# Four latent projections accumulated feature tile by feature tile as the inputs arrive

## The chip, the cores and the metric

One core of one Trainium2 chip runs the whole program. The metric is the device time of one execution in microseconds (us); less is better. The engines that matter here are TensorE (PE in the profile, with its weight loads PEld), VectorE (DVE), ScalarE (ACT), GpSimd (POOL), and SyncE (SP), whose queue issues nearly all loads from HBM.

## The reference, cut to what matters

The model is a two-layer decoder trunk on 512 tokens of 1024 features. Only the input projection of the even layer and what it feeds is touched:

```
h = rms_norm(x, ev_norm)                     # x: 512 x 1024
z = h @ w_in                                 # 1024 -> 512 + 256 + 128 + 32
u, cq, ckv, kr = split(z)                    # pooling, query latent, key/value latent, rotary key
y_pool = pool_mixer(u)                       # causal means over 2/4/8/16 tokens, then 128x128 products
q  = rms_norm(cq) @ w_q_up                   # 8 heads x (64 + 32 rotary)
kv = rms_norm(ckv) @ w_kv_up                 # 8 heads x (64 keys + 64 values)
x  = x + concat(y_pool, attention(q, k, v)) @ w_out
```

After it come a cross-attention into 256 memory tokens and a SwiGLU block, then a second layer with a gated recurrence and the same two blocks, and a final norm.

## The kernel before, in words

Activations lie with features on the 128 partitions and the 512 tokens on the free axis, so x is eight tiles of 128x512. Every float32 operand is split into a high part of reduced precision and the rest (`split` for activations, `Weights.get` for weights), and one product is three matmuls: high by high, high by low, low by high (`mm3`, lines 166 to 168, in this order). One output tile of a 1024-wide projection is thus 8 feature tiles x 3 = 24 matmuls of 128x512 into one PSUM bank. There are eight banks: two each of `mm`, `att`, `s` and `tr`.

The norm of the layer is not applied to x first. `setup` multiplies x by the gain only (line 156 on ACT, 157 on DVE) and sums the squares of x over the feature tiles into `ssq` (a square on ACT, lines 243 and 246; an add on POOL, line 247). The factor per token, `rx`, is worked out from `ssq` later (`rstd_cols`: column sums by matmul at line 183, then small DVE operations and one POOL power) and spread over the partitions by `bcast` (line 230) into `R`.

`setup` loads x tile by tile and, after every second tile, one block of `ev_w_in`. A block of this layout is one output tile: 128x1024 numbers, its eight feature tiles side by side (512 KB). Output tile by output tile, `even` makes z[0], z[1] (query latent), z[2] (key/value latent), z[3] (the 32 rotary keys and their swapped halves, twice), and later the four pooling projections in `u_tile`. Each `linear` call therefore needs all eight tiles of x and one block of weights. Raw weight blocks have two buffers, their high and low parts three each.

A table of rotary factors (`rope_table`, lines 371 to 415) is worked out on DVE and ACT from the positions in between. Behind z come the second norms (line 453: sums of squares of z), the latent for keys and values (`ck`, line 459), the rotary key (464 to 477), the pooling tiles, and the attention of four pairs of heads. The cross-attention's keys of the memory are also worked in there (`mem_gained`, `mem_keys`).

The order of the instructions on each engine is made when the program is built, by a planner that follows the program's order with its own estimates of durations and lets a later instruction go ahead of one that is not ready. `tc.issue_after(i)` holds the instructions of its block behind instruction i. On the chip each engine then keeps that order, and so does SP's queue of loads. Before anything arrives, `setup` runs 12 products of ones with ones (line 296).

Of the kernel before, what the change touches and what calls it, by code (L numbers as in the profile page):

```python
# [18 lines left out]
P = 128  # L19
T = 512  # L20
# [48 lines left out]
class Weights:  # L69
    """Streams [n, 128, F] blocks and splits each into float32r high and low parts."""  # L70
# [33 lines left out]
class Trunk:  # L104
# [23 lines left out]
    def pair(self, side, n=T):  # L128
        """High and low parts of an activation tile, from one of the two sides of the activation store."""
        return tuple(self.actp.tile([P, n], F32R, name=self.nm(f"act{side}"), tag=f"act{side}") for _ in range(2))  # L130
# [7 lines left out]
    def bank(self, tag="mm"):  # L138
        """A PSUM bank: mm and att for products, s for scores, tr for transposes and row sums."""
        if tag == "any":  # L140
            self.flip ^= 1
            tag = ("mm", "att")[self.flip]
        return self.psum.tile([P, T], F32, name=self.nm(tag), tag=tag, bufs=BANKS[tag])
# [15 lines left out]
    def mm3(self, out, terms, begin=True, end=True):  # L159
        """out = sum over terms of (wh + wl).T @ (xh + xl), less wl.T @ xl.  # L160

        A sum in pieces has its first one with begin and its last one with end."""
        nc = self.nc
        last = len(terms) - 1
        for i, (wh, wl, xh, xl) in enumerate(terms):
            nc.tensor.matmul(out, wh, xh, start=begin and i == 0, stop=False)  # L166
            nc.tensor.matmul(out, wh, xl, start=False, stop=False)  # L167
            self.mm_ins = nc.tensor.matmul(out, wl, xh, start=False, stop=end and i == last).ins  # L168

    def rstd_cols(self, *sums, inner=None, bank="tr"):  # L170
        """For each (ssq, dim, tiles, scale): [128, tiles] columns of scale * rsqrt(column sums of ssq / dim + eps).

        With inner the squared values are still to be scaled by these columns, and so is what the result scales."""
        nc = self.nc
        ps = self.bank(bank)
        n = sum(s[2] for s in sums)
        v = self.small(8)
        o = 0
        for ssq, dim, nt, _ in sums:
            terms = ssq if isinstance(ssq, tuple) else (ssq,)  # L180
            for t in range(nt):
                for i, a in enumerate(terms):
                    self.sum_ins = nc.tensor.matmul(ps[:, o + t:o + t + 1], a[:, t * P:(t + 1) * P], self.ones[:, 0:1],  # L183
                                                    start=i == 0, stop=i == len(terms) - 1).ins
            o += nt
        o = 0
        if inner is not None:
            sq = self.small(8)
            nc.vector.tensor_mul(sq[:, :inner.shape[-1]], inner, inner)
        for _, dim, nt, _ in sums:  # L190
            if inner is None:
                nc.vector.tensor_scalar(v[:, o:o + nt], ps[:, o:o + nt], 1.0 / dim, EPS, op0=ALU.mult, op1=ALU.add)
            else:
                nc.vector.scalar_tensor_tensor(v[:, o:o + nt], ps[:, o:o + nt], 1.0 / dim, sq[:, :nt],
                                               op0=ALU.mult, op1=ALU.mult)
            o += nt
        if inner is not None:
            nc.vector.tensor_scalar(v[:, :n], v[:, :n], EPS, None, op0=ALU.add)
        r = self.rsqrt(v, n)
        res, o = [], 0  # L200
        for _, _, nt, scale in sums:
            if inner is not None:
                nc.vector.scalar_tensor_tensor(r[:, o:o + nt], r[:, o:o + nt], scale or 1.0, inner,
                                               op0=ALU.mult, op1=ALU.mult)
            elif scale is not None:
                nc.vector.tensor_scalar(r[:, o:o + nt], r[:, o:o + nt], scale, None, op0=ALU.mult)
            res.append(r[:, o:o + nt])
            o += nt
        return res

    def rsqrt(self, v, n):
        """v ** -0.5 of n columns, refined by one step."""
        nc = self.nc
        y, w, r = (self.small(8)[:, :n] for _ in range(3))
        v = v[:, :n]
        nc.gpsimd.tensor_tensor(y, v, self.mhalf[:, :n], op=ALU.pow)
        nc.vector.tensor_mul(w, y, y)
        nc.vector.tensor_mul(w, w, v)
        nc.vector.tensor_scalar(w, w, -0.5, 1.5, op0=ALU.mult, op1=ALU.add)
        nc.vector.tensor_mul(r, y, w)  # L220
        return r

    def bcast(self, cols, nt=NT, bank="tr"):
        """PSUM tile [128, nt*128] with the columns' values along the free axis, on every partition."""
# [14 lines left out]
    def add_square(self, ssq, src, first):  # L239
# [4 lines left out]
        else:  # L244
            sq = self.tmp("t2", n)
            nc.scalar.activation(sq[:, :n], src, AF.Square)  # L246
            nc.gpsimd.tensor_add(ssq[:, :n], ssq[:, :n], sq[:, :n])  # L247
# [4 lines left out]
    def next_norm(self, side, gain, off):  # L252
        """State for the norm that follows a residual update: filled tile by tile."""
# [10 lines left out]
    def linear(self, W, blk, xs, off=0, bank="mm", ps=None, k0=0, k1=None):  # L264
        """One output tile: block blk of W holds its k tiles side by side. With k0 and k1 a piece of the sum."""
# [18 lines left out]
    def setup(self):  # L284
# [6 lines left out]
        # the table of the first functions is loaded before there is data  # L291
        nc.scalar.activation(self.small(1), self.ones[:, 0:1], AF.Square)
        # the array's clock is raised while the first operands are on their way
# [4 lines left out]
        nxt = self.next_norm(0, "ev_norm", 0)  # L298
        self.Win = Weights(self, ins["ev_w_in"], "evin")
        for m in range(KD):  # L300
            xt = self.actp.tile([P, T], F32, name=self.nm("xin"), tag="act1")
            nc.sync.dma_start(xt, ins["xT"][m * P:(m + 1) * P, :])
            self.feed(nxt, m, xt)
            if m in (0, 2, 4, 6):
                self.Win.get(m // 2)
# [17 lines left out]
    def mem_load(self, keys):  # L323
        """The memory, feature tiles of [128, 256], in the place of the keys to come or among the inputs."""
# [9 lines left out]
    def mem_gained(self, layer, pool, tag, keys=True):  # L334
        """The memory's norm with the layer's gain, split: feature tiles [128, 256], high and low."""
# [17 lines left out]
    def mem_keys(self, layer, mg, m0, m1, low=None):  # L353
        """Keys of the memory, [features, memory tokens]."""
# [9 lines left out]
    def rope_table(self, pool, C):  # L364
        """C: rows 0:64 one, 64:96 cos, 96:128 sin with the sign of its half.

        Worked out with 16 frequencies x 8 chunks of the positions on the partitions."""
# [49 lines left out]
    def even(self, nrm, nxt_spec):  # L417
# [4 lines left out]
        with ExitStack() as ctx:  # L422
# [10 lines left out]
            # latents: z[0:2] of the queries, z[2] of keys and values, z[3] rotary keys and their swapped halves  # L433
            z = [self.linear(Win, m, xg, bank="any") for m in range(2)]
            rx, = self.rstd_cols((nrm["ssq"], D, NT, None))
            with tc.issue_after(self.sum_ins):
                z.append(self.linear(Win, 2, xg, bank="any"))
            sq = [self.tmp(t) for t in ("t0", "t0", "t1")]
            cq = []
            for m in range(2):  # L440
# [3 lines left out]
                cq.append((h, l))  # L444
            with tc.issue_after(self.mm_ins):
                z.append(self.linear(Win, 3, xg, bank="any", k1=2))
            R = self.rp.tile([P, T], F32, name=self.nm("R"), tag="R")
            with tc.issue_after(self.mm_ins):
                row = self.bcast(rx)
            nc.scalar.activation(sq[2], z[2], AF.Square)  # L450
            nc.scalar.copy(R, row)
            with tc.issue_after(self.row_ins):
                rq, rk = self.rstd_cols(((sq[0], sq[1]), 256, NT, QKD ** -0.5), (sq[2], P, NT, None), inner=rx)
            with tc.issue_after(self.sum_ins):
                self.linear(Win, 3, xg, ps=z[3], k0=2)
# [14 lines left out]
            # queries and keys of two pairs of heads; rows 64:128 of the keys stay  # L470
# [8 lines left out]
            nc.vector.tensor_mul(CQ, self.bcast(rq), C)  # L479

            # pooling mixer
            def u_tile(g):
                ps = self.linear(Win, 4 + g, xg)
# [29 lines left out]
            # latent attention  # L513
# [22 lines left out]
            def v_pair(wh, wl):  # L536
                """Values of two heads, tokens on partitions."""
# [99 lines left out]
    def cross(self, layer, nrm, nxt_spec, mg=None):  # L637
# [3 lines left out]
        with ExitStack() as ctx:  # L641
# [40 lines left out]
            def scores(hd):  # L682
                """Softmax of one head's scores, queries on partitions, two query tiles side by side."""
# [103 lines left out]
    def odd(self, nrm, nxt_spec):  # L787
# [6 lines left out]
        with ExitStack() as ctx:  # L794
# [6 lines left out]
            # 8 * softplus(-lambda) = 8 * (max(-lambda, 0) + log1p(exp(-|lambda|)))  # L801
# [37 lines left out]
            def act(out, src, fn, **kw):  # L839
                """A function of ScalarE's tables; run() keeps those of a kind together."""  # L840
# [13 lines left out]
            def lru_gates():  # L854
                for hd in range(4):
                    if hd == 0:
                        # the row of the norm's factors comes between the first tiles
# [68 lines left out]
    def tail(self, W, ys, base, side):  # L926
        """The last projection, its residual and the final norm: features on partitions for the first tokens,
        tokens on partitions for the last ones."""
# [38 lines left out]
        def after(n):  # L967
            """The sums and the row of the norm come in between these products."""
# [46 lines left out]
def layout(inputs):  # L1015
# [21 lines left out]
    d["ev_w_in"] = con(mt(np.concatenate([z[:, 512:896], kr, ks, kr, ks, z[:, :512]], axis=1)))  # L1037
# [53 lines left out]
```

## Time and profile before

| what | us |
|---|---|
| median of 3 runs | 1421.28 |
| lowest and highest of the runs | 1419.26 and 1422.52 |
| span of the profiled execution | 1418.8 |
| PE busy in that span | 1384.2 (98%) |
| DVE, ACT, POOL busy | 784.9 (55%), 549.6 (39%), 321.7 (23%) |

The profile is of one execution; its span runs from the first to the last instruction. Nothing else is shown of that execution's own time, so what lies around the span is taken as the median less the span, 2.5 us. "Idle before" in a row is the engine's idle time ahead of the instruction, with what released it. A matmul's own time in a row includes work that overlaps with the next one; the pace is the distance from one start to the next. PEclk is the clock granted to TensorE as a share of its full speed.

### The profile page before, as it was taken

How to read it: one execution, taken by the hardware profiler on the slowest of the kernel's cores; microseconds unless marked ns; L12 is line 12 of the kernel's file. 1: busy time of each engine (PE TensorE's matmuls, PEld its weight loads, DVE VectorE, ACT ScalarE, POOL GpSimd, SP SyncE). 2: the span in 40 equal slices, each digit the busy share in tenths (PEclk: the TensorE clock that was granted, in tenths of full speed). 3: DMA queues.
4: the chain of work that ended last, by engine and by line, in shares of the span. 5: the costliest groups of instructions: out<-in, count | busy, mean ns of one | idle time of the engine just before them, and what ended most of it. 6: DMA issues, size and time to landing. Idle time of an engine off the chain costs nothing.

```text
span 1418.8 us, 16758 instructions
## 1 busy us (share of the span) xinstructions
PE 1384.2 (98%) x6524; PEld 1153.3 (81%) x6524; DVE 784.9 (55%) x1043; ACT 549.6 (39%) x859; POOL 321.7 (23%) x291
## 2 busy tenths in 40 slices
PE   8989999999999999999999989999999999999997
PEld 6878888878888888888887778888888888888887
DVE  7687574456454345344579796445545534453553
ACT  6466553454332232223434555335433312221331
POOL 4586261103110011001234470211121100110112
PEclk8999999999999999999999989999999999999999
DMA  6222162323223233332322334322323333323331
GB/s 208 75 71 79 60 193 79 115 60 118 90 90 104 89 104 92 102 90 93 108 89 90 98 105 154 96 71 91 116 89 93 100 96 98 99 84 111 93 104 60
DMA packets 45326, 140.28 MB, mean 99 GB/s; under 512 B 5568, under 2 KB 10816, under 8 KB 45248
## 3 DMA queue, kind: packets, MB, share of 16 engines
q1 hardware_dynamic: 43808, 137.91, 31.1%
q10 hardware_dynamic: 1440, 1.32, 0.3%
q8 instruction: 51, 0.84, 0.2%
q14 instruction: 27, 0.22, 0.0%
HBM read 136.98 MB, written 2.10 MB: 98 GB/s over the span
## 4 chain that ended last, share of the span: by engine, by line
PE 86%; DVE 7%; issue 2%; ACT 2%; DMA 1%; POOL 1%; POOLq 0%; SPq 0%; ACTq 0%; DVEq 0%
PE mm L166 16%; PE mm L168 16%; PE mm L167 16%; PE att L166 10%; PE att L168 10%; PE att L167 10%; DMA dn_raw<-in_ffn_down_dram 1%; DVE h L896 1%; DVE act L154 1%; PE s L166 1%; PE s L167 1%; PE s L168 1%; DVE i L895 1%; PE tr L183 1%; PE mm L667 1%
## 5 line engine op out<-in xcount | busy, mean ns | idle before, releaser
L98 ACT CAST gu_h<-gu_raw 128x1024 fp32r<-128x1024 f32 x88 | 92.8, 1054 | 293.0 <-PE mm L167 162.7
L774 POOL TENSOR_TENSOR t<-t,t 128x512 f32<-128x512 f32 x44 | 60.0, 1364 | 577.9 <-ACT gu_h L98 383.1
L99 DVE TENSOR_TENSOR gu_l<-gu_raw,gu_h 128x1024 fp32r<-128x1024 f32 x88 | 138.2, 1570 | 33.1 <-ACT gu_h L98 33.1
L166 PE MATMUL att<-act,gu_h 128*128 128x512 f32 x352 | 137.8, 391 | 0.0
L166 PE MATMUL mm<-act,gu_h 128*128 128x512 f32 x352 | 137.1, 390 | 0.0
L168 PE MATMUL att<-act,gu_l 128*128 128x512 f32 x352 | 137.0, 389 | 0.0
L167 PE MATMUL mm<-act,gu_h 128*128 128x512 f32 x352 | 136.9, 389 | 0.0
L168 PE MATMUL mm<-act,gu_l 128*128 128x512 f32 x352 | 136.9, 389 | 0.0
L167 PE MATMUL att<-act,gu_h 128*128 128x512 f32 x352 | 136.9, 389 | 0.0
L247 POOL TENSOR_TENSOR ssq<-ssq,t 128x512 f32<-128x512 f32 (+1 forms) x49 | 77.5, 1582 | 196.5 <-ACT t L246 188.5
L773 DVE TENSOR_TENSOR t<-att,R 128x512 f32<-128x512 f32 x44 | 30.4, 691 | 128.3 <-PE att L168 128.3
L98 ACT CAST dn_h<-dn_raw 128x1024 fp32r<-128x1024 f32 (+1 forms) x40 | 40.3, 1011 | 138.2 <-PE att L167 102.5
L167 PEld LDWEIGHTS att<-act,gu_h 128*128 128x128 f32 x352 | 66.2, 188 | 14.2 <-issue 0.5
L166 PEld LDWEIGHTS att<-act,gu_h 128*128 128x128 f32 x352 | 66.0, 188 | 14.1 <-issue 0.5
L168 PEld LDWEIGHTS mm<-act,gu_l 128*128 128x128 f32 x352 | 66.1, 188 | 13.9
L168 PEld LDWEIGHTS att<-act,gu_l 128*128 128x128 f32 x352 | 66.0, 188 | 13.7
L167 PEld LDWEIGHTS mm<-act,gu_h 128*128 128x128 f32 x352 | 66.0, 187 | 13.7
L166 PEld LDWEIGHTS mm<-act,gu_h 128*128 128x128 f32 x352 | 66.1, 188 | 13.5
L274 DVE TENSOR_TENSOR x<-mm,x 128x512 f32<-128x512 f32 x44 | 30.3, 690 | 83.4 <-PE mm L168 82.6
L770 DVE TENSOR_TENSOR t<-mm,R 128x512 f32<-128x512 f32 x44 | 30.4, 691 | 69.6 <-PE mm L168 66.8
L153 ACT CAST act<-t 128x512 fp32r<-128x512 f32 (+1 forms) x53 | 32.9, 621 | 71.9 <-POOL t L774 56.0
L99 DVE TENSOR_TENSOR dn_l<-dn_raw,dn_h 128x1024 fp32r<-128x1024 f32 (+1 forms) x40 | 56.2, 1408 | 6.6 <-ACT dn_h L98 6.6
(397 smaller groups left out, 3541.8 us busy)
## 6 DMA issues: line engine op xcount, KB each, us to landing
gu_raw<-in_ffn_gu_dram SPq DMA_DIRECT2D x88, 512.0 KB, 3.5
dn_raw<-in_ffn_down_dram SPq DMA_DIRECT2D x32, 512.0 KB, 3.6
xk_raw<-in_xa_w_k_dram SPq DMA_DIRECT2D x16, 512.0 KB, 3.5
xq_raw<-in_xa_w_q_dram SPq DMA_DIRECT2D x16, 512.0 KB, 3.6
xv_raw<-in_xa_w_v_dram SPq DMA_DIRECT2D x16, 512.0 KB, 3.5
xo_raw<-in_xa_w_o_dram SPq DMA_DIRECT2D x16, 512.0 KB, 3.6
odin_raw<-in_od_w_in_dram SPq DMA_DIRECT2D x16, 512.0 KB, 3.5
dn_raw<-in_ffn_down_dram SPq DMA_DIRECT2D x16, 384.0 KB, 3.0
```

The costliest lines, as they stand in the source:

```text
L98: nc.scalar.copy(hi, src)
L99: self.low.tensor_sub(lo, src, hi[:, :].bitcast(F32))
L153: nc.scalar.copy(hi, src)
L154: nc.vector.tensor_sub(lo, src, hi.bitcast(F32))
L166: nc.tensor.matmul(out, wh, xh, start=begin and i == 0, stop=False)
L167: nc.tensor.matmul(out, wh, xl, start=False, stop=False)
L168: self.mm_ins = nc.tensor.matmul(out, wl, xh, start=False, stop=end and i == last).ins
L247: nc.gpsimd.tensor_add(ssq[:, :n], ssq[:, :n], sq[:, :n])
L274: self.nc.vector.tensor_add(self.x[m], ps, self.x[m] if src is None else src)
L770: nc.vector.tensor_mul(t, pg, R)
L773: nc.vector.tensor_mul(u, pu, R)
L774: nc.gpsimd.tensor_mul(u, u, t)
```

## The change

The columns of `ev_w_in` for the four latent tiles get a layout of their own, `ev_z`: eight blocks, one for each feature tile, of 128x512 numbers (256 KB), with the four output tiles side by side. `setup` now runs through the feature tiles: it loads x tile k and block k of `ev_z`, splits both, and issues the 12 matmuls that add this feature tile to all four outputs, which stand open in the two `mm` and the two `att` banks. Three of the eight banks' roles thus change: z[0] and z[2] lie in `mm`, z[1] and z[3] in `att`. In this loop the add of the squares is done by DVE and no longer by POOL.

`even` begins with all four z done. The pooling projections, now blocks 0 to 3 of a smaller `ev_w_in` whose loads and splits are asked for in `even` alone, take the place of z[2] and z[3] as products between which the norms' sums are put: the first three feature tiles of projection 0, then the sums of the second norms, then the other five, then the row of `rx`. Projections 0 and 1 lie in the `s` banks, 2 and 3 in `mm`; 1 to 3 are written down after the rotary keys and before the pooling tiles. The number of matmuls is the same. Comments and docstrings are dropped as well.

```diff
-    def add_square(self, ssq, src, first):
+    def add_square(self, ssq, src, first, low=None):
...
-            nc.gpsimd.tensor_add(ssq[:, :n], ssq[:, :n], sq[:, :n])
+            (low or nc.gpsimd).tensor_add(ssq[:, :n], ssq[:, :n], sq[:, :n])
...
         nxt = self.next_norm(0, "ev_norm", 0)
+        Wz = Weights(self, ins["ev_z"], "evz")
+        Wz.group = 1
+        self.z = [self.bank(t) for t in ("mm", "att") * 2]
+        for k in range(KD):
+            xt = self.actp.tile([P, T], F32, name=self.nm("xin"), tag="act1")
+            nc.sync.dma_start(xt, ins["xT"][k * P:(k + 1) * P, :])
+            h, l = self.pair(0)
+            self.split(xt, h, l, scale=self.vec("ev_norm", k))
+            nxt["xg"].append((h, l))
+            wh, wl = Wz.get(k)
+            for m, z in enumerate(self.z):
+                ms = slice(m * P, (m + 1) * P)
+                self.mm3(z, [(wh[:, ms], wl[:, ms], h, l)], k == 0, k == KD - 1)
+            self.add_square(nxt["ssq"], xt, k == 0, low=nc.vector)
         self.Win = Weights(self, ins["ev_w_in"], "evin")
-        for m in range(KD):
-            xt = self.actp.tile([P, T], F32, name=self.nm("xin"), tag="act1")
-            nc.sync.dma_start(xt, ins["xT"][m * P:(m + 1) * P, :])
-            self.feed(nxt, m, xt)
-            if m in (0, 2, 4, 6):
-                self.Win.get(m // 2)
...
-            z = [self.linear(Win, m, xg, bank="any") for m in range(2)]
+            z, zins = self.z, self.mm_ins
             rx, = self.rstd_cols((nrm["ssq"], D, NT, None))
-            with tc.issue_after(self.sum_ins):
-                z.append(self.linear(Win, 2, xg, bank="any"))
...
+            nc.scalar.activation(sq[2], z[2], AF.Square)
+            R = self.rp.tile([P, T], F32, name=self.nm("R"), tag="R")
+            ups = [self.linear(Win, 0, xg, bank="s", k1=3)]
             with tc.issue_after(self.mm_ins):
-                z.append(self.linear(Win, 3, xg, bank="any", k1=2))
-            R = self.rp.tile([P, T], F32, name=self.nm("R"), tag="R")
+                rq, rk = self.rstd_cols(((sq[0], sq[1]), 256, NT, QKD ** -0.5), (sq[2], P, NT, None), inner=rx)
+            with tc.issue_after(self.sum_ins):
+                self.linear(Win, 0, xg, ps=ups[0], k0=3)
             with tc.issue_after(self.mm_ins):
                 row = self.bcast(rx)
-            nc.scalar.activation(sq[2], z[2], AF.Square)
             nc.scalar.copy(R, row)
-            with tc.issue_after(self.row_ins):
-                rq, rk = self.rstd_cols(((sq[0], sq[1]), 256, NT, QKD ** -0.5), (sq[2], P, NT, None), inner=rx)
-            with tc.issue_after(self.sum_ins):
-                self.linear(Win, 3, xg, ps=z[3], k0=2)
...
             nc.vector.tensor_mul(CQ, self.bcast(rq), C)
+            ups += [self.linear(Win, g, xg, bank="s" if g == 1 else "mm") for g in (1, 2, 3)]
             def u_tile(g):
-                ps = self.linear(Win, 4 + g, xg)
+                ps = ups[g]
...
-    d["ev_w_in"] = con(mt(np.concatenate([z[:, 512:896], kr, ks, kr, ks, z[:, :512]], axis=1)))
+    d["ev_z"] = con(np.concatenate([z[:, 512:896], kr, ks, kr, ks], axis=1).reshape(KD, P, 4 * P))
+    d["ev_w_in"] = con(mt(z[:, :512]))
```

## Rows read from the trace of the kernel before

**Rows 1.** The page: PE's busy time over the whole span, and the granted clock in 40 equal slices of 35.5 us.

```profile
PE 1384.2 (98%) x6524; PEld 1153.3 (81%) x6524; DVE 784.9 (55%) x1043; ACT 549.6 (39%) x859; POOL 321.7 (23%) x291
...
PEclk8999999999999999999999989999999999999999
```

**Rows 2.** The view by windows, the first 98 us cut into seven stretches; its columns are in its first line ("x" counts instructions).

```profile
core 0: us, PE busy (x) PEld busy (x) DVE busy (x) ACT busy (x) POOL busy (x), PEclk, DMA share, GB/s
0.00:6.40 6.40, 5.20 (x25) 5.01 (x25) 0.75 (x2) 3.89 (x6) 2.29 (x17) 1.00 0.67 235
6.40:16.80 10.40, 5.54 (x12) 2.84 (x12) 10.33 (x13) 10.02 (x17) 8.87 (x6) 0.62 0.95 360
16.80:22.60 5.80, 5.76 (x14) 4.56 (x15) 5.80 (x12) 0.57 (x2) 2.40 (x2) 0.50 0.30 90
22.60:28.00 5.40, 5.40 (x27) 4.49 (x25) 3.36 (x9) 1.94 (x5) 0.00 (x0) 1.00 0.47 132
28.00:72.00 44.00, 44.00 (x213) 36.12 (x213) 29.10 (x55) 20.07 (x35) 21.28 (x19) 1.00 0.27 81
72.00:82.00 10.00, 8.04 (x33) 5.75 (x34) 8.47 (x21) 5.88 (x12) 6.93 (x8) 0.83 0.50 167
82.00:98.00 16.00, 13.07 (x85) 10.46 (x83) 15.47 (x32) 11.54 (x32) 13.65 (x17) 1.00 0.00 1
```

**Rows 3.** The timeline of PE in its first 23 us: start, time of one, what it is, and the idle time before it with what ended it.

```profile
0.97 5.13 PE L296 MATMUL tr<-ones 128*128 128x128 f32 x24 [0.97 <-POOL ones L290]
6.33 0.50 PE L166 MATMUL att<-act,evin_h 128*128 128x512 f32 x1 [0.23 <-ACT evin_h L98]
...
8.07 0.50 PE L168 MATMUL att<-act,evin_l 128*128 128x512 f32 x1 [1.00 <-DVE evin_l L99]
...
9.93 0.79 PE L167 MATMUL att<-act,evin_h 128*128 128x512 f32 x1 [1.13 <-DVE act L157]
...
13.14 0.79 PE L167 MATMUL att<-act,evin_h 128*128 128x512 f32 x1 [1.56 <-DVE act L157]
...
16.84 0.80 PE L168 MATMUL mm<-act,evin_l 128*128 128x512 f32 x1 [1.20 <-DVE evin_l L99]
...
22.55 0.45 PE L166 MATMUL mm<-act,evin_h 128*128 128x512 f32 x1
```

**Rows 4.** The chain of work that ended last, in order of time, first 50 us: start, time on the chain, what it is.

```profile
13.01 1.30 DVE rp_l L390
...
15.65 1.14 DVE evin_l L99
...
22.32 0.43 PE mm L168
...
23.23 0.23 PE att L168
...
37.60 0.86 PE tr L230 x2
38.45 2.57 PE tr L183 x24
```

**Rows 5.** The view by windows for PE alone, from the first matmul of z[0] to the end of z[1].

```profile
6.33:27.83 21.50, 16.61 (x49) 0.68 0.65 230
```

**Rows 6.** Groups of DVE instructions between 6 and 28 us, shapes apart: count, busy time in us, mean ns of one, idle before.

```profile
L157 DVE SCALAR_TENSOR_TENSOR act<-xin,vecs,act 128x512 fp32r<-128x512 f32 x7 | 6.2, 887 | 0.0
...
L386 DVE TENSOR_SCALAR rp_q<-rp_r 128x64 f32<-128x64 f32 x1 | 1.3, 1286 | 0.0
...
L382 DVE SCALAR_TENSOR_TENSOR rp_t<-rp_q,rp_t 128x64 f32<-128x64 f32 x3 | 0.6, 210 | 0.0
```

**Rows 7.** Groups of ACT instructions between 3 and 28 us, same columns.

```profile
L156 ACT ACTIVATE act<-xin,vecs 128x512 fp32r<-128x512 f32 x8 | 5.6, 712 | 1.2 <-DMA vecs<-in_vecs_dram 1.2
L246 ACT ACTIVATE t<-xin 128x512 f32<-128x512 f32 x7 | 4.2, 620 | 0.4 <-POOL ssq L247 0.4
```

**Rows 8.** The timeline of ACT and DVE, four single instructions on tiles of 128x512: the low part of the first x tile, a weight block's high part, its low part, and the low part of the values.

```profile
4.64 0.75 DVE L157 SCALAR_TENSOR_TENSOR act<-xin,vecs,act 128x512 fp32r<-128x512 f32 x1 [4.64 <-ACT act L156]
...
60.22 0.62 ACT L98 CAST evp_h<-evp_raw 128x512 fp32r<-128x512 f32 x1
...
62.38 1.12 DVE L99 TENSOR_TENSOR evp_l<-evp_raw,evp_h 128x512 fp32r<-128x512 f32 x1
...
72.38 0.69 DVE L154 TENSOR_TENSOR vl<-att,vh 128x512 fp32r<-128x512 f32 x1
```

**Rows 9.** The issues of DMA up to 70 us: count, KB each, median us from issue to landing.

```profile
xin<-in_xT_dram SPq DMA_DIRECT2D x9, 256.0 KB, 5.2
...
evp_raw<-in_ev_pool_dram SPq DMA_DIRECT2D x1, 256.0 KB, 2.6
```

**Rows 10.** The timeline from 49 to 78 us: the copy of the row for the key/value norm, the low parts of the first two queries, the last matmul of the pooling projections, the first scores, and a matmul of the next pair's queries.

```profile
49.28 0.59 ACT L457 COPY t<-tr 128x512 f32<-128x512 f32 x1 [3.20 <-PE tr L230]
...
65.41 3.03 POOL L526 TENSOR_TENSOR act<-t,act 128x512 fp32r<-128x512 f32 x2
...
69.57 0.39 PE L168 MATMUL mm<-act,evin_l 128*128 128x512 f32 x1
...
71.97 0.53 PE L559 MATMUL s<-act,act 128*128 128x128 f32 x2
...
77.38 0.80 PE L166 MATMUL att<-cqh,evqkv_h 128*128 128x512 f32 x1 [1.00 <-DVE act L154]
```

## The prediction

> **What bounds the kernel now.** I read the page first: PE is busy 98% of the span, and two of the 40 slices show a granted clock below 9 tenths, the first and the twenty-fourth [rows 1]. So the time is PE's own work at its pace, plus what PE loses in a few places. The change keeps the number of matmuls; it can pay only where PE waits or runs slowly. The windows show that place [rows 2]: from 28 to 72 us PE is busy all the time at full clock, whereas from 6.4 to 22.6 us it ran 26 matmuls in 16.2 us at 0.62 and then 0.50 of the clock, that is mostly at 1.2 GHz. The timeline of PE says why [rows 3]. The waits ahead of 8.07, 9.93, 13.14 and 16.84 us are 1.00, 1.13, 1.56 and 1.20 us, each ended by a DVE low part, of a weight block or of an x tile. Behind these waits the clock fell, and it came back only at 22.55, when PE had run without a gap since 16.84. On the chain one matmul goes by in 0.43 us before that and in 0.23 us after [rows 4]. The pace at full clock, from starts that lie next to each other in the trace, is 0.227 us.
>
> DVE is the late one there: 10.33 of 10.40 us busy [rows 2]. Part of that is not work. A rotary-table operation on 128x64 takes 0.21 us by itself and 1.29 us while POOL adds squares [rows 6], and two of these slow ones lead into the weight split that PE then waits for [rows 4].
>
> **What it costs now.** z[0] and z[1] are 48 matmuls; with the first sum they fill 6.33 to 27.83 us [rows 5]. At full pace 48 take 48 x 0.227 = 10.9 us. So 21.5 - 10.9 = 10.6 us are lost there. z[2] and z[3], 48 more, are then done at full pace, so by PE's count all four tiles cost until 27.8 + 10.9 = 38.7 us, leaving aside the sums and rows put in between, which stay.
>
> **The loop of the change, part by part.**
>
> *PE.* Each feature tile now gives 12 matmuls that need only this tile and its block: 12 x 0.227 = 2.72 us at full pace, 12 x 0.43 = 5.2 us at half. Eight tiles are 96 x 0.227 = 21.8 us. The start: the products of ones end at 6.1 us [rows 3], and by then tile 0 is there (below). If nothing waits, z ends at 6.1 + 21.8 = 27.9 us.
>
> *ACT* per tile: the high part of x 0.71, the square 0.62 [rows 7], the high part of a 128x512 block 0.62 [rows 8]: 1.95 us, below 2.72.
>
> *DVE* per tile: the low part of x, the low part of the block, the add of squares. The add and this size of block on DVE are not in the trace without company. Bounds: 0.69 us for the same shape alone, with one operand in PSUM, and 1.12 beside POOL [rows 8]; for the x part 0.75, the time of the first tile, with POOL still idle [rows 8], and the mean of the others, 0.89 [rows 6]. With POOL out of the loop I take the lower ends: 0.75 + 0.69 + 0.69 = 2.13 us, below 2.72. The upper ends give 3.1 us, which would make DVE the bound by 0.4 us a tile. Beside the loop DVE has some 21 rotary operations at 0.21, 4.4 us, and a query weight split of 0.9. In all 8 x 2.13 + 5.3 = 22.3 us against PE's 21.8: the loop's own instructions come first in the program and the rest fills in, so I allow 0.5 us of waiting.
>
> *POOL* loses seven adds and gains nothing; nobody waits for it here.
>
> *Loads.* 16 loads of 256 KB are 4.2 MB against 2.1 MB of x and up to 2.1 MB of weights before. At the 360 GB/s that the loaded queue showed [rows 2] they take 11.7 us, 1.46 us a tile. The narrow place is the two raw buffers: block k + 2 is issued when the low part of block k is done. Landing takes 2.6 us on an empty queue and 5.2 behind others [rows 9]; with 0.62 + 0.69 for the split and about 1 us in DVE's queue a pair of buffers turns in some 4.9 us, 2.5 us a block; behind a full queue, 7.5, or 3.8 a block. SP's queue keeps its order, so the x tiles, the first query weights and the memory's four loads that go ahead of block 2 or 3 delay it. By my count block 2 lands near 9.8 us and is split by 11.3, when PE asks for it at 6.1 + 2 x 2.72 = 11.5; later blocks gain on PE unless the memory's 1 MB (2.9 us) goes in between, a wait of about 1 us at most, since of the 12 matmuls of a tile eight need no low part of the weights. With the 0.5 above I set the end of z at 28.4 us; bounds 27.9 and 33.
>
> **Behind the loop.** Let z end at E. The sums of x (0.8 us), nine matmuls of projection 0 (2.0), the 24 sums of the second norms (2.57, [rows 4]) follow without need to wait: ACT squares z[0] and z[1] while PE still adds the last tile to z[2] and z[3], and 2.8 us are left to it for the rest. The blocks of the pooling weights: the third of them waits only for a buffer freed at E, and there are 2.0 us and more of matmuls between two needs. In the row of before, 8.3 us pass from the end of those sums (41.0) to the copy for the keys' norm at 49.28 [rows 4, 10]; the same chain gives E + 5.4 + 8.3 = E + 13.7. From there the first two queries' low parts on POOL were ready 19.2 us later (68.4 against 49.28, [rows 10]): E + 32.9. PE until then has 0.8 + 2.6 sums, three rows of 0.86, 96 matmuls of pooling and 12 of queries (24.5), so E + 30.5; in the trace of before 2.4 us more go by from the last pooling matmul at 69.57 to the first scores at 71.97, hence E + 32.9. It comes out even; before there was 3.5 us to spare. I charge 0.5 us for this, with up to 2 as the far end. One weight split of 1.2 us on DVE leaves this stretch, since the pooling blocks are split earlier. The waits from 72 to 98 us, where DVE is 15.47 of 16 us busy [rows 2], move along unchanged.
>
> **The sum.** 38.7 - 28.4 - 0.5 = 9.8 us earlier at the attention, and from there on PE is the bound to the end. Against the profiled execution: 1418.8 - 9.8 = 1409.0 of span, plus 2.5 us around it, 1411.5 us; the median of before is that same 1418.8 + 2.5.
>
> **A rule that speaks against it.** After four waits of 1.0 to 1.6 us the granted clock was at 1.2 GHz for some 12 us [rows 3]. The Trainium skill, "TensorE: Matmul & The Clock Gate", section "HAM oscillation — how this bites in real kernels", describes a loop over feature tiles in which each tile's matmuls are short and PE then waits for the next load, so that every tile starts at the low clock; it advises against waiting for data inside such a loop. The trace agrees that waits bring the clock down; whether this loop waits, no row here shows. If that rule decides, it is the third rival.
>
> **Rivals.**
> 1. *DVE sets the pace or the clock falls once.* For it: DVE's total equals PE's; blocks 2 and 3 land just in time. Against: POOL is out of the way. With 3.1 us a tile DVE, which begins at 4.6 [rows 8], ends at about 4.6 + 8 x 3.1 + 2 = 31.4 us; or gaps of 1.5 us and then 14 matmuls at 0.43 instead of 0.227, as between 16.84 and 22.55 [rows 3], 2.8 us, give 32.5. Gain 6 to 7, about 1415 us.
> 2. *The gain is given back before the attention.* The first scores wait for the chain of DVE and POOL behind the rows, and the memory's norm or the rotary table is late as well: PE arrives 10 us early and stands still, falls to the low clock (as at 77.38, [rows 10]) and the time is what it was, 1420 to 1424. For it: the even balance above and DVE's full stretch. Against: nearly all of this chain hangs on z itself, which moves.
> 3. *The loop runs at the low clock from end to end.* PE begins with a tile, waits for the next, and never gets a full stretch: 96 x 0.43 = 41.3 us from 6.1, z at 47.4, against 38.7: 8.7 us slower, 1430. It decides if each tile arrives more than 5.2 us after the one before. Against: at the low clock a tile lasts 5.2 us, longer than any supply worked out above (3.8 at most), so waits end by themselves and the clock returns, as it did at 22.55.
>
> **Chances and range.** The forecast 0.73 (own range 1408 to 1414), rival 1 0.13, rival 2 0.07, rival 3 0.07. The range from 1406.5, where z ends at 27.9 and 4 of the 5 us that PE loses from 72 to 98 go too, to 1418 holds the forecast and rival 1. A difference of less than 0.2% (2.8 us) can't be told from no change: faster 0.86, same 0.07, slower 0.07.
>
> **What would show it.** Right: in the profile after, matmuls into all four z banks from about 6 us at a pace of 0.227 with the clock at 1.00, z done at 28 to 29 us, rotary operations at 0.2 us, the last pooling matmul near 59 instead of 69.57. Wrong: PE waits for the low part of a `ev_z` block or its load, a clock of 0.5 over more than 6 us of the loop, or a new wait of PE between 28 and 60 us, above all before the first scores.

## The result: nothing gained, and the profile after

The changed kernel takes 1423.74 us in the median (1421.61 to 1427.42, 18 runs), the kernel before 1421.3 beside it (18 runs): ratio 1.0019, interval 1.0012 to 1.0026. It is a little slower, 1411.5 was forecast, and the range ended at 1418. The profiled execution spans 1420.9 us, against 1418.8.

The windows of the changed kernel, cut as in [rows 2] up to 28 us and finer behind it:

```profile
6.40:22.60 16.20, 14.73 (x67) 11.61 (x65) 15.20 (x40) 11.02 (x20) 0.00 (x0) 1.00 0.84 276
22.60:28.00 5.40, 5.40 (x28) 4.54 (x28) 2.61 (x12) 3.50 (x8) 1.04 (x1) 1.00 0.61 165
28.00:60.00 32.00, 32.00 (x148) 25.73 (x147) 23.10 (x42) 15.20 (x26) 11.22 (x10) 1.00 0.30 92
60.00:72.00 12.00, 9.37 (x36) 8.09 (x35) 6.90 (x11) 5.18 (x8) 11.26 (x10) 0.69 0.24 72
72.00:84.00 12.00, 8.11 (x32) 5.85 (x32) 8.44 (x22) 5.95 (x13) 5.31 (x7) 0.78 0.22 77
84.00:98.00 14.00, 13.08 (x78) 10.18 (x77) 12.34 (x28) 10.84 (x29) 12.42 (x17) 0.96 0.04 14
```

From 6.4 to 22.6 us PE runs 67 matmuls at full clock instead of 26 [rows 2]: the gain was made. From 60 to 84 us it then idles and runs slowly where [rows 2] show it busy until 72. PE's timeline names the waits. The first line is the last pooling matmul, which started at 69.57 before [rows 10]:

```profile
59.24 0.39 PE L168 MATMUL mm<-act,evin_l 128*128 128x512 f32 x1
...
64.12 0.47 PE L166 MATMUL att<-ckh,evqkv_h 128*128 128x512 f32 x1 [2.63 <-DVE t L530]
...
70.46 0.63 PE L166 MATMUL att<-cqh,evqkv_h 128*128 128x512 f32 x1
...
78.26 0.50 PE L566 MATMUL s<-act,act 128*128 128x512 f32 x1 [1.65 <-ACT pr L640]
...
81.45 0.33 PE L566 MATMUL s<-act,act 128*128 128x128 f32 x1 [2.15 <-ACT pr L640]
```

The view by windows gives the clock behind the first wait (columns: PE busy, clock, DMA):

```profile
64.10:74.70 10.60, 10.58 (x35) 0.52 0.32 111
```

So 2.6 us are lost by waiting, some 5.1 by the half clock and 3.8 by waiting for exps, 11.5 in all. Before, 72 to 82 us lost 10 - 8.04 x 0.83 = 3.3 [rows 2]. The difference, 8.2, is nearly all of what the loop won.

To follow it I add up what PE has started by a time t: each matmul at its pace at full clock (0.227 us for 512 columns, 0.18 and 0.12 for 384 and 256, 0.11 for 128 or fewer). The lead is this sum less that of the kernel before; 8.4 us, say, is 37 matmuls of 512 columns. Beside it stand the starts of the copy for the keys' norm and of the first, seventh and thirty-first exp (eight heads, four rows each; the seventh is the second head's third row). The rows below the second belong to the experiments.

```
lead of PE over the kernel before (us) at t =              | copy  exp 1  exp 7  exp 31
                  30   60   70   85  100  120  145  160  185
before             0    0    0    0    0    0    0    0    0 | 49.3  75.4  88.9  160.6
after            8.4  8.4  2.8 -0.6  0.7  0.7  0.8 -0.8 -2.3 | 47.8  76.0  88.8  162.3
e1 queries 1st   8.6  8.6  3.9 -0.1  1.6  1.6  1.1  0.0 -1.6 | 47.5  74.6  88.5  161.5
e3 squares 1st   8.2  8.4  6.2  3.6  2.5  1.3  0.0 -1.5 -3.0 | 45.5  72.7  92.3  162.9
e4 adds only     2.7  3.0  2.3  1.2  2.8  2.2  1.1  0.1 -1.4 | 46.5  74.2  88.1  161.3
e9 POOL free     8.6  7.0  3.4  2.0  1.9  1.0  0.0 -1.4 -3.0 | 46.9  70.5  92.7  162.9
e10 e3 + casts   8.6  7.0  4.8  3.1  2.0  0.4  0.0  0.0  0.0 | 46.9  74.0  94.4  160.4
e11 all casts    8.6  7.3  3.9  3.3  2.0  1.4  1.1  1.3  1.1 | 46.7  73.9  94.3  159.3
e12 last cast    8.4  6.6  1.8 -1.4 -1.7 -1.4 -1.6 -3.2 -3.2 | 49.6  77.9  91.7  163.8
e14 + mem POOL   8.2  8.4  6.2  3.3  4.3  3.7  1.9  1.7  1.6 | 45.5  72.7  84.6  159.0
e15 + mem PE     8.4  8.4  6.2  3.1  4.8  4.8  3.0  2.8  2.7 | 45.5  72.7  84.5  157.9
e16 all orders   8.4  7.0  4.2  5.1  7.5  7.4  5.7  4.9  5.4 | 47.0  70.1  82.5  155.3
e17 before+ord.  0.2  0.5  0.2  1.2  2.5  1.3  0.4 -1.0 -1.1 | 49.0  76.7  88.2  161.9
e18 no squares   8.2  6.6  1.8  0.1 -0.5 -0.3 -0.4 -2.0 -2.0 | 49.6  73.0  89.9  162.6
```

In the changed kernel 8.4 us are there at 60 us and none at 85, where the exps come when they always came; another 3 go between 145 and 185. The lead at 185 us is what the spans differ by, to 0.7 us, but for e15, which gains 1.8 more later, and e17, whose one execution lost 4 more (mostly behind 700 us, in stages that no edit touches). The expectations below quote leads up to 1 us above this table's.

Each row is one execution, and they scatter: up to 150 us e12 has the order of the changed kernel on every engine, yet its copy comes 1.7 and its first exp 1.9 us later, after a low clock behind 39 us (last section). A landmark that differs by less than 2 us in one execution is weak evidence.

### The profile page after: what moved, and what is told of

The parts are those of the page before. It is cut to its first block, busy times and chain, and to the rows that moved or that the text cites. A ratio compares the mean times of both kernels' runs of the same rounds, so it can differ in the third digit from the quotient of the medians.

```text
span 1420.9 us, 16770 instructions
## 1 busy us (share of the span) xinstructions
PE 1384.6 (97%) x6524; PEld 1153.8 (81%) x6524; DVE 783.3 (55%) x1054; ACT 550.1 (39%) x863; POOL 310.8 (22%) x284
## 4 chain that ended last, share of the span: by engine, by line
PE 84%; DVE 8%; issue 3%; ACT 2%; DMA 2%; POOL 1%; POOLq 0%; ACTq 0%; DVEq 0%
PE mm L166 16%; PE mm L168 16%; PE mm L167 15%; PE att L166 9%; PE att L168 9%; PE att L167 9%; PE s L168 1%; PE s L166 1%; DMA dn_raw<-in_ffn_down_dram 1%; PE s L167 1%; DVE h L903 1%; DVE t L838 1%; DVE i L902 1%; DVE act L154 1%; DVE xk_l L99 1%
## 5 line engine op out<-in xcount | busy, mean ns | idle before, releaser
L247 POOL TENSOR_TENSOR ssq<-ssq,t 128x512 f32<-128x512 f32 (+1 forms) x42 | 66.5, 1582 | 209.2 <-ACT t L246 208.8
L168 PEld LDWEIGHTS mm<-act,gu_l 128*128 128x128 f32 x352 | 66.1, 188 | 13.7
```

What stands on the lines that cost most here:

```text
L247: (low or nc.gpsimd).tensor_add(ssq[:, :n], ssq[:, :n], sq[:, :n])
```

## The experiments

**First: three causes, one at a time.** DVE's timeline suggests why the first scores don't come earlier: it evicts the first query at 63.30, 14.9 us after `ck` (48.44), with a pooling tile in between:

```profile
48.44 0.75 DVE L465 SCALAR_TENSOR_TENSOR t<-mm,vecs,t 128x512 f32<-128x512 f32 x1 [1.09 <-ACT t L463]
...
57.66 2.26 DVE L506 TENSOR_TENSOR hd<-t,kc 128x16 f32<-128x16 f32 x1
59.95 0.69 DVE L508 SCALAR_TENSOR_TENSOR t<-t,pu 128x512 f32<-128x512 f32 x1
...
63.30 1.27 DVE L530 TENSOR_TENSOR t<-att,ropeC 128x512 f32<-128x512 f32 x2
```

e1 puts that tile behind the second query's eviction:

```diff
-                pool_tile(p, us[p])
+                with tc.issue_after(q0_ins) if p == 0 else nullcontext():
+                    pool_tile(p, us[p])
```

> The changed kernel with one edit: on VectorE the first pooling tile's operations are queued behind the evictions of the first two query heads. Theory A (order on VectorE): in the changed kernel TensorE runs out at 61.3 us and waits 2.63 us for a query eviction that stands behind pooling tile 0, and then runs at 1.2 GHz for 10 us; without that order the wait is under 1.0 us, the clock stays at 0.95 or more from 61 to 75 us, and the time falls by 5 to 8 us, to 1416 to 1419 us. Theory B (the first exponentials are set by something that did not move with the latents): the wait only turns up later, before the scores or the exponentials, and the time stays within 1.5 us of 1423.7.

Measured 1422.95, ratio 1.0013 (1.0004 to 1.0023). The wait of 2.63 is gone, and others take its place: 1.57 at 66.83, 1.12 at 69.31, 1.65 and 2.16 for exps at 77.36 and 80.55. At 85 us no lead is left (-0.1). That is theory B.

e2 keeps PE busy there with 12 added products that nobody reads:

```diff
+                        for _ in range(FILL):
+                            f_ins = nc.tensor.matmul(fill, cq[0][0][:, :P], cq[1][0], start=True, stop=True).ins
```

> The changed kernel with 12 extra matmuls of 128x512 (2.7 us at full clock, their result is not used) on TensorE between the first two query heads and the first keys, where it waits 2.63 us. Theory C (the clock is the larger part of the loss): the clock stays at 1.00 from 64 to 75 us and the time falls by 4 to 5 us, to about 1419. Theory A alone (the wait itself is the loss) or theory B: the time stays within 1.5 us of 1423.7.

1421.42, ratio 0.9995 (0.9986 to 1.0005): 2.3 us below the changed kernel although PE does 2.7 us more, between the two theories. The clock stays at 1.00 until 72 us, then PE waits 3.60 us for the first exps (from 74.4). So a part of the loss is the clock's own, and the rest turns from slow running into waiting: PE has nothing that could be done yet.

e3 goes for the start of the norms' chain. In the changed kernel ACT meets a weight cast that waits for its load ahead of the squares of z; PE's sums of them come at 36.56:

```profile
31.57 1.05 ACT L98 CAST evin_h<-evin_raw 128x1024 fp32r<-128x1024 f32 x1 [2.39 <-DMA evin_raw<-in_ev_w_in_dram]
32.53 0.59 ACT L448 ACTIVATE t<-mm 128x512 f32<-128x512 f32 x1
```

```diff
-            ups += [self.linear(Win, g, xg, bank="s" if g == 1 else "mm") for g in (1, 2, 3)]
+            with tc.issue_after(sq2_ins):
+                ups += [self.linear(Win, g, xg, bank="s" if g == 1 else "mm") for g in (1, 2, 3)]
```

> The changed kernel with the splits of pooling blocks 1 to 3 queued on ScalarE behind the squares of the latents. In the changed kernel ScalarE waits 2.4 us at 29.2 us for the load of block 1 while the latents are done. Theory D (the chain of the norms is late from its start): the sums of the second norms end at 37 instead of 38.9 us, the copy of the row for the keys' norm comes near 46 instead of 47.8, TensorE waits about 0.6 instead of 2.6 us, and the time falls by 2 us, or by up to 7 if the clock holds. Theory B: no more than 1.5 us either way.

1424.21, ratio 1.0024 (1.0014 to 1.0034), no faster. But the profile shows more than the time: the sums come at 33.42 instead of 36.56, copy and first exp 2 to 3 us earlier, and 3.6 us of lead are there at 85. They go afterwards.

e4 is the kernel before with only the square adds of `setup` on DVE (`low=nc.vector`).

> The kernel before with one part of the change alone: the squares of x are added by VectorE instead of GpSimd. If GpSimd's adds are what makes the first VectorE operations slow, the rotary operations take 0.21 instead of 1.29 us, the four waits of TensorE before 17 us shrink to half or less and z[1] ends 3 to 6 us before 27.8. Theory A or D: the norms' chain hangs on z and comes earlier with it, and the time falls by 2 to 5 us against 1421.3. Theory B: within 1.5 us of 1421.3.

1421.71, ratio 1.0003 (0.9993 to 1.0012). The rotary operation of 1.29 us [rows 6] takes 0.19 there, as the prediction had read it, and the lead is 3.0 at 60 us, -1.4 at 185. This gain, made in another way, goes the same way.

**Second: is it POOL?** POOL is nearly full from 60 to 72 us (11.26 of 12 us above). e5 is e1 and e3 together. On top of it e6 puts the memory's low parts behind the queries' low parts, e8 has the first edit of the diff below, and e9 both.

> The changed kernel with both orders mended (the first pooling tile on VectorE behind the second query's eviction; the splits of the later pooling blocks on ScalarE behind the squares). Theory of the order: together they return at least half of the 10 us, 1414 to 1418. Theory of GpSimd: the first queries' low parts still end there at 68 to 69.5 us, after 2.85 us each for the memory's low parts ahead of them, and the first exp is no earlier than 71; the time stays at 1421 to 1425.

> The same, and the memory's two low parts on GpSimd queued behind the first two queries' low parts. Theory of GpSimd: the low parts end at 62 to 65 us instead of 68 to 69, the first scores and exps come 4 us earlier, and the time falls to 1416 to 1420. Theory that the loss is only passed on to whatever is due next: the memory's keys are then late, TensorE waits or slows down 5 to 6 us as before somewhere between 72 and 120 us, and the time is within 1.5 us of the run with both orders mended.

> Both orders mended, and the memory's square adds on VectorE instead of GpSimd (8 adds of 0.7 to 1.1 us leave GpSimd from 48 us on). Theory of GpSimd: its queue is some 6 us shorter by 60 us, the memory's low parts and then the queries' low parts end 3 to 5 us earlier, 1416 to 1420. Rival, VectorE is the one that binds between 48 and 75 us: it gets 4 to 6 us more work and the time is 1422 to 1427.

```diff
-                self.add_square(ssq, mem[m], m == 0)
+                self.add_square(ssq, mem[m], m == 0, low=nc.vector)
...
-                nc.gpsimd.tensor_sub(ql, t, qh[:, :].bitcast(F32))
+                (nc.vector if h < 2 else nc.gpsimd).tensor_sub(ql, t, qh[:, :].bitcast(F32))
```

> The last one, and the first two queries' low parts on VectorE too: GpSimd has nothing left that the first scores wait for. Theory of GpSimd: first scores by 66 us, first exp by 68, loss of TensorE between 60 and 98 us under 6 us (12.6 in the changed kernel), 1412 to 1418. If VectorE binds, or if the loss is passed on further down, 1420 to 1426.

e5 1425.04 (1.0021 to 1.0047), e6 1429.53 (1.0044 to 1.0074), e8 1426.84 (1.0029 to 1.0059), e9 1422.84 (1.0002 to 1.0021). None is faster. e8 lies in the range of its rival, VectorE; e6 missed both of its ranges, and why it is the slowest is not shown. As the only cause POOL falls: in e9 the first exp comes 4.9 us earlier than in the kernel before, at 70.5. Yet the seventh comes 3.8 later than there (in e5, e6 and e8 8 to 10 later). Between the sixth and the seventh something stops the heads.

**Third: what stands ahead of the seventh exp.** ACT's timeline of e3:

```profile
80.47 0.46 ACT L641 ACTIVATE pr<-s,sx 128x256 f32<-128x256 f32 x1
...
86.64 1.04 ACT L98 CAST xk_h<-xk_raw 128x1024 fp32r<-128x1024 f32 x1 [2.14 <-PE mm L167]
...
91.06 1.05 ACT L98 CAST xk_h<-xk_raw 128x1024 fp32r<-128x1024 f32 x1 [2.23 <-PE mm L167]
92.01 0.37 ACT L371 COPY keys<-mm 128x256 f32<-128x256 f32 x1
92.28 0.59 ACT L641 ACTIVATE pr<-s,sx 128x384 f32<-128x384 f32 x1
```

Two casts of the memory's key weights wait for a buffer that PE still reads, and the exp stands behind them in ACT's fixed order. The same picture stands at the end of the attention of the changed kernel, where the thirty-first exp comes 1.7 us later than before:

```profile
161.05 1.05 ACT L98 CAST evout_h<-evout_raw 128x1024 fp32r<-128x1024 f32 x1 [2.82 <-PE mm L167]
162.01 0.36 ACT L371 COPY keys<-mm 128x256 f32<-128x256 f32 x1
162.27 0.58 ACT L640 ACTIVATE pr<-s,sx 128x384 f32<-128x384 f32 x1
```

e10 is e3 with the first pair of casts held behind the exps of the first two heads, e11 also the other cast behind the last head's; e12 is the changed kernel with the last alone, e13 is e9 with both.

```diff
-                    self.mem_keys(0, mg, 2 * p - 2, 2 * p, nc.gpsimd)
+                    with tc.issue_after(exp_ins) if p == 2 else nullcontext():
+                        self.mem_keys(0, mg, 2 * p - 2, 2 * p, nc.gpsimd)
...
+            if first and m == 2:
+                with self.tc.issue_after(self.max_ins), self.tc.issue_after(self.exp_ins):
+                    W.get(base + m)
```

> The kernel with the squares first (the later pooling blocks' splits on ScalarE behind the squares; 1424.2 us), and the casts of the third and fourth block of the memory's key weights on ScalarE queued behind the exps of the first pair. In that kernel the seventh exp waits from 81 to 92 us behind two of these casts, which wait for a weight buffer that TensorE still reads; TensorE's lead over the kernel before falls there from 4 us at 85 to 1 at 145 us. Theory of the queue (the gain is lost where weight casts stand ahead of exps in ScalarE's order): the seventh exp comes at 83 to 86 us, the lead at 120 us is 4 us or more, and the time is 1419 to 1422. Rival, the lead is lost for want of other work for TensorE, whatever the order on ScalarE: 1423 to 1426.

> The same, and the cast of the third output-projection block queued behind the last head's exps. In every variant so far that cast, waiting for the memory's last products, stands ahead of the last head's third and fourth exp, and TensorE loses some 3 us against the kernel before between 140 and 185 us. Theory of the queue: exps 31 and 32 come 1.5 to 3 us earlier, and the time is 1.5 to 3 us below the run without it (1416 to 1420). Rival, want of other work: within 1 us of it.

> The changed kernel with only that output-projection cast queued behind the last head's exps. Theory of the queue: 1.5 to 3 us below the changed kernel, 1420.5 to 1422.5, its profile unchanged up to 150 us. Rival: 1423 to 1425.

> The kernel with nothing on GpSimd ahead of the first scores (1422.8 us), with both casts queued behind the exps. Theory of the queue: its seventh exp was 3.8 us later than in the kernel before although the sixth was 3.2 earlier, so 3 to 5 us come back and 1.5 to 3 more at the end: 1415 to 1419. Rival: 1421 to 1424.

e10 1420.95 (0.9988 to 1.0006), e11 1420.11 (0.9981 to 1.0000), e12 1422.60 (0.9996 to 1.0015), e13 1421.31 (0.9985 to 1.0004): each 0.8 to 3.3 us below its base, but only e10's interval lies clear of its base's (e3). e10's time is in the range of its theory by luck: its seventh exp comes at 94.4 instead of 83 to 86, its lead at 120 us is 0.4 instead of 4, and what it gains on e3 it gains behind 145 us (0.0 throughout, where e3 falls to -3.0). e11 and e12 lie between theory and rival, e13 in its rival's range.

Nor is the last cast the main thing. In the kernel before it stands in the same place (first line, ACT), after a short wait. In e12, where it is gone, the copy waits for the memory's products instead (second line):

```profile
159.29 1.05 ACT L98 CAST evout_h<-evout_raw 128x1024 fp32r<-128x1024 f32 x1 [0.64 <-PE mm L167]
```

```profile
163.58 0.37 ACT L374 COPY keys<-mm 128x256 f32<-128x256 f32 x1 [2.96 <-PE mm L168]
```

The thirty-first exp comes 4.7 us behind the thirtieth there, 5.5 in the changed kernel: the cast is 0.8 us of it. The seventh exp stays at 94.3 in e11, so the casts weren't the only thing ahead of it. POOL's timeline of e11 shows the next:

```profile
78.15 6.98 POOL L360 TENSOR_TENSOR keys<-keys,Rmem 128x256 f32<-128x256 f32 x8
85.11 0.75 POOL L649 TENSOR_SCALAR pr<-pr,sx 128x384 f32<-128x384 f32 x1
```

The first head's third row is normalised behind eight multiplications of the memory. Its transposes wait, on PE behind 24 products of the memory's keys as well, and the cast of the transposed rows stands on ACT ahead of the seventh exp (91.45, idle 3.09 before it). e14 holds POOL's multiplications behind the first head's normalisations, e15 also PE's first products of the memory behind that head's transposes, and e16 moves the two low parts to DVE as in e9:

```diff
-            nc.gpsimd.tensor_mul(mem[m], mem[m], self.Rmem)
+            with self.tc.issue_after(self.hold):
+                nc.gpsimd.tensor_mul(mem[m], mem[m], self.Rmem)
...
+                    with tc.issue_after(exp_ins if p == 2 else self.hold_pe) if p < 3 else nullcontext():
```

> The kernel with both casts queued behind the exps (1420.1 us), and the memory's eight multiplications on GpSimd queued behind the last normalisation of the first head. There the first head's third and fourth rows were normalised at 85 to 89 us, behind these multiplications, and its transposes, the seventh exp (94.3, 5.4 us later than in the kernel before) waited for them. Theory of the queues: the rows are normalised by 81 us, the seventh exp comes by 89, TensorE's lead at 120 us is 3 us or more instead of 2.0, and the time is 1418 to 1419.5. Rival, want of other work for TensorE: the memory's products are late instead and the time is 1420 or more.

> The same, and the memory's first products on TensorE queued behind the first head's transposes. Theory of the queues: the transposes no longer stand behind 24 products, another 0.5 to 1.5 us. Rival: TensorE idles ahead of the transposes, no gain or up to 2 us slower than without.

> The same, and the first two queries' low parts on VectorE instead of GpSimd. Theory of the queues: first exp 2 to 3 us earlier than without, 1416 to 1418.5. Rival, VectorE is full there: no gain.

e14 1419.09 (0.9976 to 0.9994), e15 1418.40 (0.9964 to 0.9993), e16 1415.21 (0.9944 to 0.9973). Each step alone is hardly more than the intervals; the three together, 4.9 us from e11 to e16, are clear of them. All three came as their theories had it, e16 0.8 us below its range. The seventh exp comes at 84.6, 84.5 and 82.5, and more of the lead is carried through: 5.4 us at 185. The windows of e16:

```profile
60.00:72.00 12.00, 9.62 (x55) 8.03 (x54) 11.08 (x17) 7.63 (x14) 11.26 (x8) 1.00 0.48 142
72.00:84.00 12.00, 9.32 (x54) 6.79 (x52) 11.18 (x28) 8.96 (x24) 9.87 (x13) 1.00 0.09 24
84.00:98.00 14.00, 13.28 (x98) 11.79 (x97) 13.38 (x25) 9.21 (x22) 13.46 (x13) 1.00 0.08 21
```

207 matmuls against 146 in the changed kernel, at a clock of 1.00 throughout.

**Last: the change or the orders?** e17 gives e16's orders to the kernel before, e18 leaves out of e16 only e3's line, and e19 is e16 again.

> The kernel before the change with the same orders in its attention (the two casts behind the exps, the memory's multiplications behind the first head's normalisations, its first products behind that head's transposes, the first two queries' low parts on VectorE). If the orders only let through the 10 us that the change won at the start, they are worth little here, where 10.3 us are lost at the start: 1419.5 to 1422.5. Rival, the orders are a gain of their own and the change has no part in it: 1415 to 1417.

> The changed kernel with these orders, but with the pooling blocks' splits on ScalarE left ahead of the squares, so that the norms' chain starts as late as in the changed kernel (copy for the keys' norm at 47.8 us instead of 45 to 46). Theory of the queues: the first exps come 2 us later than with the squares first, 1416 to 1418.5. Rival, the start of that chain doesn't matter once the queues are in order: within 1 us of the kernel with all of them.

> The kernel with all the orders once more, for a narrower interval and beside the last two on one chip: 1414.5 to 1416.

e17 1423.56 (1.0007 to 1.0025), 1 us above what I expected; e18 1421.74 (0.9992 to 1.0012), slower than either theory had it; e19 1415.79 (0.9950 to 0.9974). The orders alone gain nothing: the 6 us that e16 and e19 win on the kernel before are part of the change's own 8.4, let through (the lead of e16 is never above 8.4). And they need the squares first: without them the 6 us are gone again (first query evicted at 65.8 instead of 62.5), and the squares first alone (e3) gave none. How the 2.6 us of the copy in e18 grow to 6 is not shown, nor where the other 3 of the 8.4 go in e16.

## Why the prediction was wrong

- **The loop: right.** All four z come at a pace of 0.23 us and full clock, with one wait of 1.37 us at 16.12, for a block whose load took 6.4 us from issue to landing (5.2 had been counted). z ends at 31.2 instead of 28.4 (mostly the wait, and 0.8 of sums that moved in), inside the bounds. Of 10.3 us of lead forecast there, 8.4 were made. Rival 3 fell; the rule on loops over feature tiles (the Trainium skill, "TensorE: Matmul & The Clock Gate", "HAM oscillation — how this bites in real kernels") did not decide, since PE hardly waited.
- **"Behind the loop": the step that failed.** These lines of the changed kernel (PE, PE, ACT, POOL) are the wait, the sums, the copy and the two low parts:

```profile
16.12 0.50 PE L166 MATMUL mm<-act,evz_h 128*128 128x512 f32 x1 [1.37 <-ACT evz_h L98]
...
36.56 2.51 PE L183 MATMUL tr<-ones,t 128*128 128x1 f32 x22
...
47.82 0.59 ACT L463 COPY t<-tr 128x512 f32<-128x512 f32 x1 [1.37 <-PE tr L230]
...
66.67 2.55 POOL L533 TENSOR_TENSOR act<-t,act 128x512 fp32r<-128x512 f32 x2
```

  "E + 13.7" for the copy, 42.1, was 47.82: z 2.8 later; 2.5 more to the end of the sums, because "without need to wait" left out ACT's cast in front of the squares: PE's order has 22 products of projection 0 ahead of most sums instead of the nine counted (in e3, without that cast, it is nine, and the sums end at 36.15 instead of 39.07); the rest in the chain behind. From there to the low parts on POOL 21.4 us passed instead of 19.2. They were forecast for 61.3 and end at 69.2, no earlier than the 68.4 of before. "It comes out even", with 0.5 charged and 2 as the far end, was the term that was mis-sized: 9.0 us of lead go between 60 and 85 us. My error of kind: I counted the matmuls left to PE and took the other engines' chain to move along with z. It hung on z by its data, but on the engines' orders by its place. With five of these orders changed and two operations moved (e16), 5.4 of the 8.4 us reach 185 us.
- **"The waits from 72 to 98 us move along unchanged": wrong as well.** Exps, normalisations and transposes stood behind the memory's casts, multiplications and products, and what a variant saved before 85 us it lost behind it (e3, e9).
- **Rival 2 is what happened**, with its range (1420 to 1424), at a chance of 0.07. What spoke "against" it, that nearly all of the chain hangs on z, was no evidence.

## What to carry to other kernels

A gain on the busiest engine lasts until that engine next needs something from the others. Before counting it to the end, follow that chain through each engine's order and ask what stands ahead of each link: here weight casts that waited for buffers, a pooling tile, and the memory's multiplications. Mending one place often moved the loss to the next; the landmarks (exp by exp) showed steps working while the total stood still, and in e10 a total that fell without the step working.

## What I had not expected of the hardware

The clock fell without any idle time of PE. In e16 it is at 0.59 from 37 to 40 us, mostly the lower of its two levels (1.2 GHz), just behind the norms' sums of one column each, with PE busy throughout. In e15, with the same sums, it stays at 1.00 (PE's timeline of e16, then the windows with PE busy, clock, DMA, e16 first):

```profile
33.29 2.73 PE L183 MATMUL tr<-ones,t 128*128 128x1 f32 x24
```

```profile
34.00:37.00 3.00, 3.00 (x22) 0.84 0.13 19
37.00:40.00 3.00, 3.00 (x9) 0.59 0.70 246
```

```profile
34.00:37.00 3.00, 3.00 (x24) 1.00 0.13 19
37.00:40.00 3.00, 3.00 (x15) 1.00 0.70 246
```

9 of the 17 profiled executions with the changed kernel's loop have such a dip, and some 1.5 us less lead at 60 us (7.0 against 8.4 in the table), which is part of the scatter of single profiles. That the sums bring it about is not shown: eight executions have them and no dip.

And small DVE operations can be long: in the changed kernel the one on 128x16 takes between 0.16 and 2.26 us, by the view of one tile (ns: least, median, most):

```profile
L506 DVE TENSOR_TENSOR hd<-t,kc x4: 159/234/2261, 57.7 to 114.2; 128x16 f32<-128x16 f32 x4
```

The long one ends at 59.92; POOL's low part of a memory weight block beside it (from 57.03, 2.85 us) ends at 59.88. The Trainium skill, "SBUF — State Buffer", "Who interferes with whom", calls the port pair that VectorE and GpSimd share an exclusive lock; this pair of rows agrees.
